# Wide token projections with tokens stationary and 512 weight columns moving, and a gated sum that is transposed

## The chip, the core and the metric

The kernel runs on one core of one Trainium2 chip. The metric is the device time of one execution in microseconds (us). Three runs of the kernel before gave 2199.41, 2200.2 and 2200.22 us.

## What is computed

Two layers of a first block (256 tokens, width 1024), each a token mixer and then a feed-forward net (dense in the first layer, 8 experts with top 2 in the second), and two hybrid layers behind it. All is float32. What the change touches:

```python
def token_mixer(...):             # layer a0, a1
    z = xn @ w_in                 # 7168 columns: pool, conv, sgu, q k v, 4 x 1024 gates
    ...                           # y_a, y_b, y_c: 256 wide; y_d (attention): 512 wide
    gates = sigmoid(z[..., OFF_GATE:])
    merged = (gates[:, :, 0] * (y_a @ w_branch_pool) + gates[:, :, 1] * (y_b @ w_branch_conv)
              + gates[:, :, 2] * (y_c @ w_branch_sgu) + gates[:, :, 3] * (y_d @ w_branch_attn))
    return merged @ w_out

def hybrid_layer(x, mem, ...):    # layer b0, b1
    proj = rmsnorm(x, pre_g) @ w_in          # 13 parts; z, sb_v, ret_v, ret_g are 512 wide
    y_ret = retention(ret_q, ret_k, ret_v) * silu(ret_g)
    y_ssd = ssd_mixer(xbc, z, ...); y_sb = stick_breaking(...) * silu(sb_g)
    y_mem = memory_read(mem_q, rmsnorm(mem), w_mem_kv) * silu(mem_g)   # keys, values: 512 wide each
    return x + rmsnorm(concat(y_ret, y_ssd, y_sb, y_mem) @ w_out, post_g)
```

## The kernel before

The program is a stream of weight tiles of [128, 2048] float32 (1 MB) in a fixed order (`weight_plan`), in the stages a0, ffn, a1, moe, b0, b1. Each is loaded by a DMA of SP, and split in two: H = the tile rounded to fp32r (ACT, `wh`), L = tile - H (DVE, `wl`). The activations are split likewise. A product is three fp32r matmuls: H by H, L by H, H by L. Tiles split ahead lie in a ring of three pairs of H and L; `ahead` issues the next tile's H in the middle of a tile and `lows` its L at the tile's end, so that a DVE queue reads: L of the next tile, then what empties the present one.

A tile is used in one of two ways. In `proj_w` the weights are stationary and 256 tokens move (`mm_w`): out is [columns, tokens]. In `proj_t` the tokens are stationary and 256 weight columns move (`mm_t`): out is [tokens, columns]. A tile holds all 8 row blocks of 256 columns and takes 48 matmuls of 256 columns, into one PSUM bank. `mm_t` is also used with 512 columns moving, by the sums over w_out, w_down and the like (`add`, `tail`).

PSUM has 8 banks in four rings of two: "ps" (the stream's projections, in turn), "ac" and "ad" (side work, sums), "tr" (transposes).

A layer of the first block (`layer_a`): the tile sv, emptied by a gelu of ACT; q, k, v by two tiles each (`proj_t`), emptied by a scaled copy of ACT; su, pa, cc, ch, cb (`proj_w`); then the gates of the four branches, four tiles each (`proj_w`, tanh on ACT), with the branches' own products between them. `branch(b)` multiplies (tanh + 1) by the product (DVE) and adds it to `mg` (GpSimd; in the last branch two of four on DVE). `mg` has columns on the partitions, so that each of its quarters is split (H, L) as it stands, one quarter behind the other, and becomes the moving side of w_out. The short convolution: zc = cc * ch, three taps into yc, yc * cb, all on DVE but one tap.

A layer of the second block (`layer_b`): z (2 tiles, `proj_t`), x, then in the order `sq sk mq sv rq rk rv sg mg rg` two tiles each; sv and rv by `proj_t`, the rest by `proj_w`. The gate of the retention, rg, has columns on the partitions, and multiplies the transposed result out of PSUM.

The memory's values (`mem_kv`, parts 2 and 3, `proj_t`) are a filler: their tiles run on PE at the start of moe and of b1, while the norm and the router are worked out. At the start of moe PE takes, between matmuls of these tiles: 16 transposes of x, the router's 16 matmuls (`ac<-hT,grw`), two small transposes of its logits (`tr<-cst,lT`), ten small ones with the masks (`tr<-sm,cst`), and then the gather of the first expert's tokens (`tr<-sel,xr`).

Attention, pooling, the gating unit and so on are side work: generators whose steps `tick` puts into the queues between the matmuls, where a rough model of the engines (`Clock`) expects their operands. So where a step stands may change with anything ahead of it.

Of the kernel before, what the change touches and what calls it, by code (L numbers as in the profile page):

```python
# [23 lines left out]
# for the bits of -v / 2: its sign and its exponent are in the shifted bits  # L24
MAGIC = 1597463007 + (1 << 30) - (1 << 22)

# ---------------------------------------------------------------- layouts by shape
# columns of "cols" (one value per partition)
# [31 lines left out]
# rows that are sent to all partitions  # L60
# [6 lines left out]
# constants  # L67
# [5 lines left out]
def _constants():  # L73
# [11 lines left out]
    # part A: 1/count of the pooling windows, the exchange matrix, one-hot buckets  # L85
# [15 lines left out]
    # part B: decays of the retention and the rotary tables  # L101
# [18 lines left out]
# ---------------------------------------------------------------- order of the weights  # L120
def _rg(a, n):
    return [(a, a + n)]


def weight_plan():
    """Tiles of [128, 2048] in the order of use: (array, index, first row block, row blocks, column ranges)."""
# [12 lines left out]
    def layer_a(l):  # L139
        put(("a", l, "sv"), "w_in", (l,), 0, 8, _rg(1280, 256))  # L140
        for nm, c0 in (("q", 1536), ("k", 2048), ("v", 2560)):
            for i in range(2):
                put(("a", l, nm, i), "w_in", (l,), 0, 8, _rg(c0 + 256 * i, 256))
# [3 lines left out]
        def gates(b):  # L147
            for i in range(4):
                put(("a", l, "g", b, i), "w_in", (l,), 0, 8, _rg(3072 + b * 1024 + 256 * i, 256))
# [20 lines left out]
    def memkv(l, *parts):  # L170
        for p in parts:
            put(("b", l, "mkv", p), "w_mem_kv_2", (l,), 0, 8, _rg(256 * p, 256))

    def layer_b(l):
        def p(nm, i, c0):
            put(("b", l, nm, i), "w_in_2", (l,), 0, 8, _rg(c0 + 256 * i, 256))
# [46 lines left out]
# where in the last expert the memory is taken up again  # L223
LATE = 3
KV0 = (0,), (1,), (2, 3)
IN_COLUMNS = dict(sq=3592, sk=4104, sv=4616, rq=0, rk=512, rv=1024, mq=5640, sg=5128, rg=1536, mg=6152)
IN_ORDER = "sq sk mq sv rq rk rv sg mg rg"
# [7 lines left out]
# ---------------------------------------------------------------- order of the side work  # L235
# [10 lines left out]
class Clock:  # L246
    """A rough clock of the engines while the program is traced: it says when an operand will be there, so that
    side work is put into the queues at a place where it doesn't hold up the stream of the weights."""
# [33 lines left out]
    def when(self, needs):  # L282
        """needs: operands, or "tag" / "tag2" for one or two free banks"""
# [70 lines left out]
# ---------------------------------------------------------------- the program  # L354
class Prog:
# [19 lines left out]
    # ---- small helpers  # L375
# [10 lines left out]
    def psb(self, tag):  # L386
        """a bank; "ac": of both rings in turn, while these aren't apart"""
# [18 lines left out]
    def rsqrt(self, src, n, scale, eng=None):  # L406
        """1 / sqrt(src * scale + eps), by Newton's steps"""
# [23 lines left out]
    def split(self, src, scale=None):  # L431
        """H + L of src [128, 512] * scale, both fp32r."""
        H, L = self.h(F32R, "sH"), self.h(F32R, "sL")
        self.split_to(H, L, src, scale)
        return H, L
# [9 lines left out]
    # ---- side work: generators that advance between the matmuls of the stream. They yield the operands that their  # L445
    # next step takes from other engines (or False while there is nothing to do yet).
# [5 lines left out]
    def step(self, t):  # L452
        """one step of a task; False if it can't go on yet"""
# [22 lines left out]
    def until(self, cond):  # L476
        """the steps that it takes until cond() holds"""
# [10 lines left out]
    # ---- the stream of the weights: tiles as they are, in a ring or wherever there is room, then as H and L  # L488
# [62 lines left out]
    def ahead(self, n=None, later=False):  # L551
        """splits the next n tiles (as many as fit beside the one in use), loads the ones behind them.
        later: the last one's L waits for lows(), so that DVE doesn't wait for H"""
# [34 lines left out]
    def next_steps(self):  # L588
        """the split of the next tile, in four parts"""
# [20 lines left out]
    def mm_w(self, out, W, X, nk, ncols, c0, k0=0, start=True, stop=True):  # L610
        """out [128 columns, 256 tokens] += W[:, c0:c0+128]^T x^T"""
# [11 lines left out]
    def mm_t(self, outs, W, X, nk, ncols, t, k0=0, start=True, stop=True, c0=0):  # L623
        """outs[i] [128 tokens of t, <=512 columns] += x W; the columns of the outs follow each other"""
# [17 lines left out]
    def four_apart(self):  # L642
        """four others; "ac" and "tr" stay free for side work"""
# [3 lines left out]
    def add(self, acc, key, X, k0=0, start=False):  # L647
        """acc[tokens][columns] += x W for 256 of the rows of W"""
# [9 lines left out]
    def tail(self, acc, steps, after):  # L658
        """the last of those sums, (key, X, k0) each: one half of the tokens first, then the other. Yields a half
        when it is done. after: how many tiles behind them are split before."""  # L660
# [40 lines left out]

    def keep(self, ps, name):
# [4 lines left out]
    def transposed(self, blocks, tag="tr"):  # L707
        """a bank of four transposed [128, 128] blocks"""
# [5 lines left out]
    # ---- rms norm of [256, 1024] rows; transposed, as H and L  # L714
    def norm_rows(self, x, rows):
        """adds to x what rows gives; each half's rows normalised"""
# [22 lines left out]
    def start_T(self, x, g):  # L739
        """for the first layer: the rows transposed before their norm, their scales, and after them, in steps,  # L740
        the rows with their norm"""
# [45 lines left out]
    def finish_T(self, block, g, X, tags=("tr", "tr")):  # L787
        """the transposed rows, two banks at a time: an engine takes one while the other has the other"""
# [23 lines left out]
    # ---- set up  # L812
# [25 lines left out]
    def load_row(self, src, n):  # L838
        """src: a row of n*512 values in DRAM, sent to all partitions."""
# [8 lines left out]
    # ---- first block  # L848
# [1265 lines left out]
```

## Time and profile before

| | us |
|---|---|
| median of three runs | 2200.2 |
| span of the profiled execution | 2197.8 |
| PE busy in it | 2173.0 (99%) |
| DVE busy | 1693.3 (77%) |
| ACT busy | 1398.2 (64%) |
| GpSimd busy | 139.0 (6%) |
[...]
| bytes moved by DMA | 558 MB, 254 GB/s in the mean |

The profiled execution is told by its span, 2.4 us below the median. Busy times of PE are sums of durations that overlap; the pace of matmuls is read from start to start. In the rows of the timeline a bracket at the end gives the time that the engine was idle before the instruction, and what released it. All instructions carry the line of one recording helper (L320), so they are told apart by the names of what they write and read.

### The profile page before, as it was taken

The numbers are of one execution on the slowest core, as the hardware profiler recorded it, in microseconds if no ns is written. First come the engines' busy times: TensorE is split into PE (matmuls) and PEld (weight loads), VectorE is DVE, ScalarE is ACT, GpSimd is POOL, SyncE is SP. The second block draws the span as 40 slices with busy tenths as digits, with TensorE's granted clock in tenths as the row PEclk, the third lists the DMA queues.
The fourth block names the chain that finished last, engine by engine and source line by source line (L and its number), as shares of the span: only waits on it lengthen the run. The fifth ranks groups of instructions, "written<-read, shape, count | busy, mean of one in ns | idle before, by whom it ended". The sixth has DMA issues, their size and how long they took to land. (4 is left out here: it accounts for less than half of the span.)

```text
span 2197.8 us, 34889 instructions
## 1 busy us (share of the span) xinstructions
PE 2173.0 (99%) x13470; PEld 1944.1 (88%) x13470; DVE 1693.3 (77%) x2242; ACT 1398.2 (64%) x1869; POOL 139.0 (6%) x159
## 2 busy tenths in 40 slices
PE   8999999999999999999999999999999999999998
PEld 8999999999998888888888888888877999989997
DVE  6675755567657889898989989898998767777765
ACT  6644544465445777777778777777776656455652
POOL 2003000100030000000000000000000022101300
PEclk9999999999999999999999999999999999999999
DMA  7445455544467999999999999999966444544342
GB/s 285 154 172 192 174 190 192 197 171 159 167 229 296 371 353 355 353 357 353 369 344 355 370 356 356 346 361 355 365 267 256 172 151 154 182 154 168 121 136 103
DMA packets 138140, 558.39 MB, mean 254 GB/s; under 512 B 15720, under 2 KB 16112, under 8 KB 88816
## 3 DMA queue, kind: packets, MB, share of 16 engines
q1 hardware_dynamic: 134928, 547.63, 68.0%
q0 software_dynamic: 2176, 6.90, 0.9%
q8 instruction: 108, 1.77, 0.3%
q10 hardware_dynamic: 864, 1.57, 0.2%
q14 instruction: 64, 0.52, 0.1%
HBM read 554.98 MB, written 1.06 MB: 253 GB/s over the span
## 5 line engine op out<-in xcount | busy, mean ns | idle before, releaser
L320 DVE TENSOR_TENSOR wl<-w,wh 128x2048 fp32r<-128x2048 f32 (+1 forms) x300 | 682.0, 2275 | 213.6 <-ACT wh L320 209.5
L320 ACT ACTIVATE wh<-w 128x2048 fp32r<-128x2048 f32 (+1 forms) x300 | 567.0, 1892 | 73.5 <-issue 36.1
L320 PE MATMUL ps<-xH,wh 128*128 128x256 f32 x1728 | 493.7, 286 | 2.1 <-PEq L1433 2.1
L320 PE MATMUL ps<-xL,wh 128*128 128x256 f32 x1728 | 489.3, 283 | 0.6 <-issue 0.4
L320 PE MATMUL ps<-xH,wl 128*128 128x256 f32 x1728 | 489.0, 283 | 0.1
L320 PE MATMUL ps<-wh,sH 128*128 128x512 f32 x944 | 377.0, 403 | 0.0
L320 PE MATMUL ps<-wh,sL 128*128 128x512 f32 x944 | 366.4, 392 | 0.0
L320 PE MATMUL ps<-wl,sH 128*128 128x512 f32 x944 | 364.8, 390 | 0.0
L320 PEld LDWEIGHTS ps<-xH,wh 128*128 128x128 f32 x1728 | 331.3, 192 | 5.2 <-issue 3.8
L320 PEld LDWEIGHTS ps<-xL,wh 128*128 128x128 f32 x1728 | 331.4, 192 | 1.6 <-DVE xL L320 0.8
L320 DVE TENSOR_TENSOR wl<-wraw,wh 128x512 fp32r<-128x512 f32 x536 | 331.2, 687 | 1.7 <-ACT wh L320 1.6
L320 PEld LDWEIGHTS ps<-xH,wl 128*128 128x128 f32 x1728 | 331.2, 192 | 0.9 <-issue 0.5
L320 ACT ACTIVATE wh<-wraw 128x512 fp32r<-128x512 f32 x536 | 293.2, 622 | 10.3 <-PE ac L320 10.2
L320 DVE TENSOR_TENSOR wl<-wm,wh 128x2048 fp32r<-128x2048 f32 x88 | 201.6, 2291 | 27.1 <-ACT wh L320 25.5
L320 PEld LDWEIGHTS ps<-wh,sL 128*128 128x128 f32 x944 | 177.1, 188 | 39.3
L320 PEld LDWEIGHTS ps<-wl,sH 128*128 128x128 f32 x944 | 177.8, 188 | 34.3 <-DVE wl L320 0.4
L320 PEld LDWEIGHTS ps<-wh,sH 128*128 128x128 f32 x944 | 177.3, 188 | 33.0
L320 ACT ACTIVATE wh<-wm 128x2048 fp32r<-128x2048 f32 x88 | 168.5, 1916 | 16.6 <-PE ac L320 12.4
L320 PE MATMUL ad<-wh,a 128*128 128x512 f32 x448 | 174.6, 390 | 1.8 <-DVE a L320 1.3
L320 PE MATMUL ac<-wh,a 128*128 128x512 f32 x448 | 174.3, 389 | 0.0
L320 PE MATMUL ps<-wh,xH 128*128 128x256 f32 x448 | 130.2, 291 | 1.3 <-ACT wh L320 1.3
L320 PE MATMUL ps<-wl,xH 128*128 128x256 f32 x448 | 128.9, 288 | 2.1 <-DVE wl L320 2.0
(436 smaller groups left out, 3053.8 us busy)
## 6 DMA issues: line engine op xcount, KB each, us to landing
w<-in_wts_dram SPq DMA_DIRECT2D x296, 1024.0 KB, 4.9
wraw<-in_wts_dram SPq DMA_DIRECT2D x536, 256.0 KB, 6.2
wm<-in_wts_dram SPq DMA_DIRECT2D x88, 1024.0 KB, 5.4
mem<-in_mem_dram POOLq DMA_DIRECT2D x12, 256.0 KB, 5.7
x<-in_x_dram SPq DMA_DIRECT2D x2, 512.0 KB, 4.5
w<-in_wts_dram SPq DMA_DIRECT2D x4, 256.0 KB, 7.3
br<-scr POOLq DMA_DIRECT2D x4, 256.0 KB, 7.1
row<-in_post_dram ACTq DMA_DIRECT2D x4, 256.0 KB, 5.3
```

The source lines that it names most:

```text
L320: r = f(*args, **kw)
```

## The change

q, k, v, the gates, z, sv, rv, rg and the memory's values now use `proj_t2`: tokens stationary, 512 weight columns moving. Two tiles make up what two tiles did, but each holds 4 row blocks of 512 columns. Both "ps" banks are held, one for each half of the tokens (t), and are written in turn, 12 matmuls each: t 0 and t 1 by the first tile, t 0 and t 1 by the second. The banks are emptied behind the second tile. The branches' tiles go the same way (24 matmuls of 512 columns), so `mg` has tokens on the partitions. All four additions of the last branch are on DVE. `turned` transposes the sum, column half by column half, 8 transposes each, and splits it out of PSUM: the first half behind branch 3, the second behind the first w_out tile. The retention's gates are multiplied before the transposes. attn scales q and k in one step.

```diff
+    def proj_t2(self, key, X, tag="ps"):
+        ps = [self.psb(tag) for _ in range(2)]
+        for i in range(2):
+            W = self.W(key + (i,))
+            for t in range(2):
+                self.mm_t([ps[t]], W, X, 4, 512, t, k0=4 * i, start=i == 0, stop=i == 1)
+                if t == 0:
+                    self.ahead(later=True)
+                    if i == 0:
+                        self.tick()
+            self.lows()
+            if i == 0:
+                self.tick()
+        return ps
...
         def gates(b):
-            for i in range(4):
-                ps = self.proj_w(("a", l, "g", b, i), X)
-                th[b, i] = self.h(F32, "th")
-                S.activation(th[b, i], ps, AF.Tanh, scale=0.5)
+            for j in range(2):
+                for t, ps in enumerate(self.proj_t2(("a", l, "g", b, j), X)):
+                    th[b, j, t] = self.h(F32, "th")
+                    S.activation(th[b, j, t], ps, AF.Tanh, scale=0.5)
                 self.tick()
+        def turned(j):
+            for kp in range(2):
+                ps = self.transposed([mg[j][t][:, (2 * kp + kk) * 128:(2 * kp + kk) * 128 + 128]
+                                      for kk in range(2) for t in range(2)])
+                M.append(self.split(ps, scale=0.5))
         def branch(b):
             self.until(lambda: b in self.Y)
...
+            def gated(j, t, ps):
+                t_ = th.pop((b, j, t))
                 V.scalar_tensor_tensor(t_, t_, 1.0, ps, op0=ALU.add, op1=ALU.mult)
...
-                    (V if b == 3 and i > 1 else G).tensor_tensor(mg[i], mg[i], t_, op=ALU.add)
-                if i == 1 or b == 3 and i == 3:
-                    self.ahead()
-                if b == 3 and i:
-                    mg[i - 1] = self.split(mg[i - 1], scale=0.5)
-            if b == 3:
-                mg[3] = self.split(mg[3], scale=0.5)
+                    (V if b == 3 else G).tensor_tensor(mg[j][t], mg[j][t], t_, op=ALU.add)
...
+            else:
+                for j in range(2):
+                    W = self.W(("a", l, "b", b, j))
+                    for t in range(2):
+                        ps = self.psb("ac" if t else "ps")
+                        self.mm_t([ps], W, self.Y[b], 4, 512, t)
+                        gated(j, t, ps)
+                        if t == 0:
+                            self.ahead(later=True)
+                    self.lows()
+                    if j == 1:
+                        turned(0)
...
         for i in range(n):
-            self.add(acc, ("a", l, "o", i), M, 2 * i, start=i == 0)
+            self.add(acc, ("a", l, "o", i), self.halves(M[i]), start=i == 0)
+            if i == 0:
+                turned(1)
...
     def mem_kv(self, l, *parts, tag="ps"):
         for p in parts:
             self.until(lambda: l in self.XM)
-            ps = (self.proj_w if p < 2 else self.proj_t)(("b", l, "mkv", p), self.XM[l], tag)
-            self.kv[l, p] = self.keep(ps, "mkv")
+            if p < 2:
+                self.kv[l, p] = self.keep(self.proj_w(("b", l, "mkv", p), self.XM[l], tag), "mkv")
+            elif p == 2:
+                for mb, ps in enumerate(self.proj_t2(("b", l, "mkv", 2), self.XM[l], tag)):
+                    self.kv[l, 2 + mb] = self.keep(ps, "mkv")
```

Three places show how the change stands in the queues. First, DVE at the end of branch 3 in layer a0, where `th` is a product or a sum of the branches, `wl` the L of a weight tile and `sL` that of a quarter of the sum. Before:

```order
L320 SCALAR_TENSOR_TENSOR sL_2555<-th_1277,sH_2554 128x512
L320 SCALAR_TENSOR_TENSOR th_2373<-th_2373,ad_2558 128x512
L320 TENSOR_TENSOR th_1470<-th_1470,th_2373 128x512
L320 TENSOR_TENSOR wl_2586<-w_2310,wh_2585 128x2048
L320 SCALAR_TENSOR_TENSOR sL_2592<-th_1357,sH_2591 128x512
L320 SCALAR_TENSOR_TENSOR sL_2596<-th_1470,sH_2595 128x512
```

and now:

```order
L329 SCALAR_TENSOR_TENSOR th_1785<-th_1785,ps_1893 128x512
L329 TENSOR_TENSOR th_1231<-th_1231,th_1785 128x512
L329 SCALAR_TENSOR_TENSOR th_1787<-th_1787,ad_1911 128x512
L329 TENSOR_TENSOR th_1233<-th_1233,th_1787 128x512
L329 TENSOR_TENSOR wl_1909<-w_1753,wh_1908 128x2048
L329 SCALAR_TENSOR_TENSOR sL_1935<-tr_1929,sH_1934 128x512
L329 SCALAR_TENSOR_TENSOR sL_1944<-tr_1938,sH_1943 128x512
```

The first quarters' L stood ahead of the branch's last product; now the first L of the sum, which the first w_out tile reads, stands behind the last product, its addition and the L of a weight tile.

Second, DVE around the tile cb in layer a0 (`p` and `sm` are softmax, `zc` and `yc` the convolution, `ps` in the row of `yc` the tile cb). Before, where the L of cb stands further ahead, in front of a division:

```order
L320 SCALAR_TENSOR_TENSOR p<-ac,B 128x512
L320 TENSOR_REDUCE sm<-p 128x2
L320 SCALAR_TENSOR_TENSOR p<-ad,B 128x512
L320 TENSOR_REDUCE sm<-p 128x2
L320 TENSOR_TENSOR wl<-w,wh 128x2048
L320 TENSOR_TENSOR zc<-cs,ps 128x2x256
L320 SCALAR_TENSOR_TENSOR yc<-zc,cols,yc 128x256 x4
L320 TENSOR_TENSOR wl<-w,wh 128x2048
L320 TENSOR_TENSOR yc<-yc,ps 128x512
```

and now:

```order
L329 SCALAR_TENSOR_TENSOR p<-ad,B 128x512
L329 TENSOR_REDUCE sm<-p 128x2
L329 SCALAR_TENSOR_TENSOR p<-ac,B 128x512
L329 TENSOR_REDUCE sm<-p 128x2
L329 TENSOR_TENSOR wl<-w,wh 128x2048 x2
L329 TENSOR_TENSOR zc<-cs,ps 128x2x256
L329 SCALAR_TENSOR_TENSOR yc<-zc,cols,yc 128x256 x4
L329 TENSOR_TENSOR wl<-w,wh 128x2048
L329 TENSOR_TENSOR yc<-yc,ps 128x512
```

The L of cb has moved behind the third set of logits, so that two Ls stand there; ahead of these rows the order also has the gating unit's product now, which stood far behind before.

Third, PE at the start of moe, around the small transposes with the masks. Before:

```order
L320 MATMUL ps_7286<-wl_7214,xH_2630 128x256
L320 MATMUL ps_7286<-wh_7213,xL_2631 128x256
L320 MATMUL tr_7305<-sm_7258,cst_79 128x8 x5
L320 MATMUL ps_7286<-wh_7213,xH_2628 128x256
L320 MATMUL ps_7286<-wl_7214,xH_2628 128x256
L320 MATMUL ps_7286<-wh_7213,xL_2629 128x256
```

and now:

```order
L329 MATMUL ps_5899<-wh_5926,xH_1978 128x512
L329 MATMUL ps_5899<-wl_5927,xH_1978 128x512
L329 MATMUL ps_5899<-wh_5926,xL_1979 128x512
L329 MATMUL tr_6045<-sm_6006,cst_79 128x8 x5
L329 MATMUL tr_6059<-sel_6056,xr_5814 128x128
L329 MATMUL tr_6059<-sel_6056,xr_5815 128x128
```

30 matmuls of the filler followed the small transposes before the gather; now the gather follows them directly.

## Rows read from the trace of the kernel before

**Rows 1.** The page, part 1: busy us, share of the span, instructions.
```profile
PE 2173.0 (99%) x13470; PEld 1944.1 (88%) x13470; DVE 1693.3 (77%) x2242; ACT 1398.2 (64%) x1869; POOL 139.0 (6%) x159
```

**Rows 2.** Pieces of the chain that ended last: start, length, engine, tile, count.
```profile
1750.36 23.03 PE ps L320 x192
...
1773.39 0.87 PE tr L320 x8
...
2181.25 8.17 PE ps L320 x36
```

**Rows 3.** The page, part 5: group, out<-in, shapes, count, busy, mean ns, idle.
```profile
L320 PE MATMUL ps<-wh,sH 128*128 128x512 f32 x944 | 377.0, 403 | 0.0
```

**Rows 4.** Timeline at sv and q, layer a0: start, length, engine (PE, ACT), instruction.
```profile
18.93 0.28 PE L320 MATMUL ps<-wh,xH 128*128 128x256 f32 x1
...
22.35 0.84 ACT L320 ACTIVATE vg<-ps,sm 128x256 f32<-128x256 f32 x2
```

**Rows 5.** Timeline of DVE, layer a0, from cc to cb.
```profile
78.89 0.69 DVE L320 SCALAR_TENSOR_TENSOR p<-ac,B 128x512 f32<-128x512 f32 x1 [1.62 <-PE ad L320]
...
81.54 0.23 DVE L320 RECIPROCAL sm<-sm 128x4 f32<-128x4 f32 x2
...
84.28 2.29 DVE L320 TENSOR_TENSOR wl<-w,wh 128x2048 fp32r<-128x2048 f32 x1
86.48 0.22 DVE L320 RECIPROCAL sm<-sm 128x2 f32<-128x2 f32 x2
...
88.45 0.69 DVE L320 SCALAR_TENSOR_TENSOR p<-ac,B 128x512 f32<-128x512 f32 x1
...
98.97 0.68 DVE L320 TENSOR_TENSOR yc<-yc,ps 128x512 f32<-128x512 f32 x1
```

**Rows 6.** Timeline of PE, layer a0: a logit pair up to the next matmul; first gates matmul.
```profile
77.72 0.48 PE L320 MATMUL ac<-qkT 64*128 64x256 f32 x1
...
78.80 0.39 PE L320 MATMUL ps<-xH,wh 128*128 128x256 f32 x1
...
94.56 0.28 PE L320 MATMUL ps<-xH,wh 128*128 128x256 f32 x1
```

**Rows 7.** Timeline of layer a1: zc and yc on DVE, first gates matmul on PE.
```profile
524.31 0.68 DVE L320 TENSOR_TENSOR zc<-cs,ps 128x512 f32<-128x512 f32 x1
...
526.53 0.28 PE L320 MATMUL ps<-xH,wh 128*128 128x256 f32 x1
...
529.98 0.68 DVE L320 TENSOR_TENSOR yc<-yc,ps 128x512 f32<-128x512 f32 x1
```

**Rows 8.** Timeline of DVE, layer a0, at the end of branch 3.
```profile
224.29 0.68 DVE L320 SCALAR_TENSOR_TENSOR th<-th,ad 128x512 f32<-128x512 f32 x1
225.01 0.69 DVE L320 TENSOR_TENSOR th<-th 128x512 f32<-128x512 f32 x1
225.62 2.28 DVE L320 TENSOR_TENSOR wl<-w,wh 128x2048 fp32r<-128x2048 f32 x1
227.82 1.29 DVE L320 SCALAR_TENSOR_TENSOR sL<-th,sH 128x512 fp32r<-128x512 f32 x2
```

**Rows 9.** Timeline of PE and DVE at the start of moe.
```profile
686.19 0.28 PE L320 MATMUL tr<-cst,lT 8*128 8x8 f32 x2
...
688.20 2.73 DVE L320 SCALAR_TENSOR_TENSOR xr<-x,sm,row 128x512 f32<-128x512 f32 x4
690.85 2.28 DVE L320 TENSOR_TENSOR wl<-wm,wh 128x2048 fp32r<-128x2048 f32 x1
...
693.99 2.48 DVE L320 TENSOR_TENSOR wl<-wraw,wh 128x512 fp32r<-128x512 f32 x4
...
694.81 1.61 PE L320 MATMUL tr<-sel,xr 128*128 128x128 f32 x13
```

**Rows 10.** Start of b1: timeline of PE; a stretch's busy us, PEclk, DMA share.
```profile
1955.81 0.63 PE L320 MATMUL tr<-cst,xr 128*128 128x128 f32 x4 [1.59 <-DVE xr L320]
...
1959.00:1961.00 2.00, 2.00 (x11) 2.00 (x11) 1.85 (x5) 1.78 (x6) 0.00 (x0) 0.50 0.71 291
```

## What is predicted, before it ran

> **What bounds the kernel now.** I read the page's busy shares first: PE is busy 99% of the span [rows 1]. A busy PE need not be at its pace, since its matmul durations overlap, so the second view is the chain of work that ended last, which in the stages that the change touches runs through PE almost alone. Its merged pieces give the pace from start to start: 192 matmuls of 256 columns in 23.03 us, 0.120 us each; 36 of 512 columns in 8.17 us, 0.227 us each; 8 transposes in 0.87 us, 0.11 us each [rows 2]. The 512-column form in the stage of that piece is one of tokens stationary and weights moving already (its group is in [rows 3]), so the form that the change brings has its pace in this trace. Third, I read the timelines of DVE, ACT and PE where the tiles of the change begin and end, for what stands between a tile's last matmul and the freeing of its PSUM bank. PE hardly waits there now, so what the change takes off PE comes off the time, and each wait that it makes is added in full.
>
> **The matmuls.** A 1 MB tile was 48 matmuls of 256 columns: 48 x 0.120 = 5.76 us. It is now 24 of 512: 24 x 0.227 = 5.45 us. Per layer that holds for 6 tiles of q, k, v, 16 of gates, 5 of branches, 8 of z, sv, rv, rg and 2 of memory values: 37, in two layers 74. 74 x 0.31 = 22.9 us less. [...] Bytes, DMA issues and the splits by ACT (H) and DVE (L) are the same in number. The transposed sum adds 16 transposes per layer, 32 x 0.11 = +3.5 us on PE. First balance: **-19.4 us**.
>
> [...]
>
> **What the change makes PE wait for.** A pair of tiles holds both "ps" banks from its first 2.72 us (12 matmuls) on. The bank used last before it was needed again after 5.76 us, now after 2.72 us. Most tiles are emptied within a microsecond by one ACT or DVE instruction. These places are not:
>
> - sv to q, first layer: q's first matmul starts at 18.93, and the gelu that empties sv's bank ends at 22.35 + 0.84 = 23.19 [rows 4], since it waits for the norm's scale. The bank is now wanted at 18.93 + 2.72 = 21.65: **+1.5 us**. Nothing in that chain moves.
> - cb to gates, both layers. cb is multiplied into yc by DVE, behind a 2.28 us L of the next tile; that ends 98.97 + 0.68 = 99.65, 5.1 us after cb [rows 5, 6], in the second layer 4.1 us after it [rows 7]. With 2.72 allowed, 2.4 and 1.4 us are the plain extrapolation. But the order also puts softmax later against the tiles and, in the first layer, the sgu work earlier. From the middle of pa's tile on DVE has there: three sets of logits (2.65 each, 78.89 to 81.54), two divisions (2.74 and 1.97), the sgu product (some 1.5, an estimate from its two shapes) and two Ls (2.2 each), 18.6 us from 1.2 us on, to 19.8 us [rows 5]. PE has in the meantime three logit pairs (1.08 each [rows 6]), sgu (some 1.1), two and a half tiles of 5.76: 18.8 us, and then wants cb's L: about +0.9. Next comes zc, behind one more L of DVE, whose H stands on ACT behind the last exponentials and a copy: some 3.6 us after the third logits at 17.6 (an estimate), so L 21.2 to 23.4 and zc at 23.4; from zc to the end of yc are 6.35 us (524.31 to 530.66 [rows 7]), so 29.7; wanted at 18.8 + 0.9 + 5.8 + 2.7 = 28.2: +1.5. In the second layer the second logits come half a tile later than before, at 10.8 us after su; 14.4 us of the same pieces follow, zc at 25.2, end 31.6; cb ends at 26.3 (three and a half tiles, three pairs, from the same rows: 20.2 + 3.2, and 2.9 of the half tile), so wanted at 29.0: +2.6. Together **+5.0 us** (0 to 7).
> - Branch 3 to the first w_out tile, both layers. Now three quarters of the sum are split when branch 3 ends, and PE goes on at once. After it, w_out needs the transposed sum split as L, and DVE has in front of that: product, sum and a 2.28 us L (as in [rows 8]). From the end of branch 3: 0.2 (the way to DVE, an estimate) + 0.72 + 0.61 + 2.20 + 0.65 = 4.4 us. PE fills 0.9 with 8 transposes (counted above) and 0.9 with the four matmuls that want H alone: 4.4 - 1.8 = 2.6, with the semaphore 2.7. Twice: **+5.4 us**. The nearest cover would be an L that is through before (then 0.5 each); at the other end 3.5 each.
> - Start of moe. The router's masks follow the small transposes at 686.19, and 30 matmuls of the second memory tile stood between the next small ones and the selection; DVE's rows of xr (2.7 us), an L, and the selection were hidden by them [rows 9]. Now 36 matmuls of 512 stand ahead of 686.19 (8.2 instead of 4.3 us: 690.0) and only 12 behind it. DVE: 688.20 + 3.85 = 692.05, xr to 694.7, an L in four pieces (2.48) to 697.2, selection 0.94: 698.1. PE is there at 690.2 + 2.7 + 1.1 (ten small ones at 0.11) = 694.0: **+4.1 us** (2 to 6).
> [...]
> - Start of b1: the two value tiles only fill the wait for the norm, which ends when it ends [rows 10]: their gain of **0.6 us** is not had.
> - Retention's gates are now multiplied before the transposes (8 small instead of 4 wide DVE instructions, far ahead of their use), attn scales q and k together, and one branch's additions go from POOL to DVE while DVE has room: nothing, covered by PE's next tiles; if the cover is gone, one eviction, about 1 us. Side work that the planner puts elsewhere: **+1.0 us** (-1 to +3).
>
> Sum: -19.4 + 1.5 + 5.0 + 5.4 + 4.1 + 1.3 + 0.6 + 1.0 = **-0.5 us**. The span was 2197.8, so 2197.3; the median lay 2.4 above the profiled span, so **2199.7 us**: no change that can be measured (a measurement of this kernel tells 0.2%, 4.4 us, from none).
>
> **Rivals.**
> (A) The waits come only in part: DVE is less behind than I count, so that cb and the router find their operands. For it: DVE is busy 77% and stands idle before many Ls for ACT. Against it: the queues are strictly in the order shown. Without cb, moe and its clock: -19.4 + 1.5 + 5.4 + 0.6 = -11.9, so 2188; with no wait at all 2181. Chance 0.25.
> (B) Slower: the second bank of every pair comes late. The place is the end of all 32 pairs (16 per layer; the branches are no pairs), the price the time by which its eviction passes 2.72 us. Without sv, cb and the unknown 1.0 the sum is -8.0 us, so it decides from 8.0 / 32 = 0.25 us per pair; at 0.5 us it is +8.0, so 2208. For it: an L of 2.28 us ahead of an eviction of 0.7 alone ends 3.2 us after the tile. Against it: most evictions are ACT's, and their L is through before the tile ends. Chance 0.17.
> (C) The change does not shorten the matmuls: if time went by columns alone, 512 would take 2 x 0.120 and only the costs would stay, 3.5 + 1.5 + 5.0 + 5.4 + 4.1 + 1.3 + 1.0 = +21.8: 2222. The two paces speak against it [rows 2]. [...] Chance 0.03.
> The forecast keeps 0.55.
>
> **How the numbers follow.** Likeliest: 2199.7. The single costs add to about -7 and +7 at their bounds, hardly all at one end. With 0.25 on A, whose times lie at 2181 to 2195, and 0.20 on B and C, the range of 8 in 10 is 2191 to 2207. Faster by over 0.2%: 0.25 (A); within: 0.55; slower: 0.20 (B, C).
>
> **What would show it.** In the changed profile: 12 matmuls of 512 columns in 2.72 us in q, gates and z (else the first term is wrong); idle PE of 1.5 us in q's first tile, released by ACT's gelu; of some 2.5 us at cb and the first gates, released by DVE; of 2 us and more four matmuls into the first w_out tile, released by sL; of 4 us ahead of the selection's transposes, released by sel, with a granted clock of 0.5 behind it. I am wrong if PE's busy time fell by much more than it waits (A), or if "ps" matmuls wait at most pairs (B).

## The result, and the profile of the changed kernel

The changed kernel took **2211.7 us** in the median (2210.2 to 2214.6) against 2200.2 before: 1.0055 of its time, 95% interval 1.0040 to 1.0069. It is slower, and lies 4.7 us above the range that was predicted. The profiled execution has a span of 2210.2 us, 12.4 more than the 2197.8 of before.

The first row below is PE's share on the page (as in [rows 1]): 6.2 us less busy, and yet a longer span. The second is the stretch in which PE runs the four gate tiles of one branch in layer a0, all of the new form (the columns are those of the table of stretches below; x97 counts one matmul that reaches in from before). The first of their 96 matmuls of 512 columns starts at 152.12, and what follows them at 173.88: 21.76 us, 0.227 us each as in [rows 2], 5.44 us a tile, at the full clock. So the tiles did become shorter by what was worked out.

```profile
PE 2166.8 (98%) x11726; PEld 1859.4 (84%) x11726; DVE 1694.6 (77%) x2250; ACT 1398.1 (63%) x1863; POOL 121.7 (6%) x155
```

```profile
152.12:173.88 21.76, 21.76 (x97) 18.02 (x96) 11.10 (x7) 9.36 (x7) 0.00 (x0) 1.00 0.55 194
```

PE's starts at the borders of the stages, read from its timeline, say where the time went. The last column is what the terms of the prediction make of each stage, without the 1.0 us of side work that it gave no place.

| stage | before us | after us | difference | terms on record |
|---|---|---|---|---|
| first mixer (first w_in matmul to ffn) | 235.81 | 237.05 | +1.24 | 0.0 |
| ffn | 201.55 | 201.62 | +0.07 | 0 |
| second mixer | 228.67 | 230.21 | +1.54 | -1.3 |
| start of moe, to the first gathered tokens | 30.48 | 35.57 | +5.09 | +4.8 |
| experts, to b0's transposes | 999.26 | 1000.41 | +1.15 | 0 |
| b0, to b1's transposes | 247.12 | 247.54 | +0.42 | -2.5 |
| b1, to PE's end | 235.84 | 238.74 | +2.90 | -2.5 |
| together | | | +12.41 | -1.5 |

Next are all the places in the timeline of PE, from the second tile on, where the changed kernel waits over 1.2 us, but for the starts of b0 and b1 (z, and b1's transposes). Those wait nearly as long in the kernel before, z there in five short pieces. The columns are start, length, instruction and, in brackets, the idle time ahead of it and what ended it. (That idle time counts from a matmul's modelled end. From start to start, beyond the pace, the waits are some 0.16 to 0.2 us longer: 2.17 us for the row with 2.00. The text gives these.)

```profile
23.22 0.50 PE L329 MATMUL ps<-wh,xH 128*128 128x512 f32 x1 [1.49 <-ACT vg L329]
...
99.84 0.50 PE L329 MATMUL ps<-wh,xH 128*128 128x512 f32 x1 [1.29 <-DVE yc L329]
...
222.88 0.50 PE L329 MATMUL ac<-wh,sL 128*128 128x512 f32 x1 [2.00 <-DVE sL L329]
...
530.66 0.68 PE L329 MATMUL ps<-wh,xH 128*128 128x512 f32 x1 [2.23 <-DVE yc L329]
531.14 0.63 PE L329 MATMUL ps<-wl,xH 128*128 128x512 f32 x1
531.57 0.63 PE L329 MATMUL ps<-wh,xL 128*128 128x512 f32 x1
532.00 0.63 PE L329 MATMUL ps<-wh,xH 128*128 128x512 f32 x1
...
655.61 0.50 PE L329 MATMUL ac<-wh,sL 128*128 128x512 f32 x1 [2.00 <-DVE sL L329]
...
701.00 2.25 PE L329 MATMUL tr<-sel,xr 128*128 128x128 f32 x11 [3.78 <-DVE sel L329]
...
1707.80 0.36 PE L329 MATMUL ps<-xH,wh 128*128 128x256 f32 x1 [2.29 <-PEq L1487]
...
1856.35 0.39 PE L329 MATMUL ps<-xH,wh 128*128 128x256 f32 x1 [1.67 <-ACT rv L329]
...
2107.14 0.39 PE L329 MATMUL ps<-xH,wh 128*128 128x256 f32 x1 [1.73 <-ACT rv L329]
```

The first six are those of the prediction, each at its place, by its releaser and nearly at its size: sv to q 1.65 (1.5 predicted), cb 1.45 and 2.39 (2.4 and 2.6), the transposed sum 0.47 + 2.17 in both layers (2.7), the selection 3.92 (4.1). The seventh, the branch ahead of the last part of moe, was there before. The last two, at the pair of rv in each hybrid layer, nobody had counted.

The second thing to see is in the three rows behind 530.66: matmuls of 512 columns start 0.43 us apart, not 0.227. The table of stretches has the granted clock behind seven waits (columns: stretch, its length, busy us of PE, PEld, DVE, ACT, POOL, granted clock, DMA share, GB/s):

```profile
224.00:227.00 3.00, 3.00 (x11) 2.41 (x11) 0.00 (x0) 0.00 (x0) 0.00 (x0) 0.50 0.73 306
531.00:534.00 3.00, 3.00 (x8) 2.32 (x8) 1.59 (x2) 2.07 (x2) 0.00 (x0) 0.50 0.92 317
658.00:660.00 2.00, 2.00 (x6) 1.61 (x5) 0.35 (x1) 0.00 (x0) 0.00 (x0) 0.50 1.05 396
702.00:704.00 2.00, 2.00 (x11) 2.00 (x11) 0.00 (x0) 0.00 (x0) 0.00 (x0) 0.50 1.05 385
1709.00:1711.00 2.00, 2.00 (x11) 2.00 (x11) 0.67 (x4) 2.00 (x5) 0.00 (x0) 0.50 1.04 434
1968.00:1971.00 3.00, 3.00 (x8) 2.28 (x9) 2.70 (x8) 2.66 (x7) 0.00 (x0) 0.50 0.74 232
2108.00:2111.00 3.00, 3.00 (x14) 3.00 (x15) 2.02 (x1) 2.65 (x2) 0.00 (x0) 0.50 0.66 221
```

The kernel before has, after its first 16 us, one such stretch, at b1's start [rows 10]. The changed one has seven. A busy PE hides this: it reads 3.00 of 3.00 us busy there, with 8 matmuls of 512 columns where 13 would fit.

So the theory to test was: **the saving was had, the waits came as worked out, two more came at rv, and six more stretches at half clock, at some 1 to 1.75 us each, are what the sum lacked.** Its rivals: the waits are not what sets the time (DVE or ACT is the bound there, and a wait taken away comes back one tile later), or the clock falls for another reason than the waits.

### The profile page after: what moved, and what is told of

The parts are those of the page before. It is cut to its first block, busy times and chain, and to the rows that moved or that the text cites. A ratio compares the mean times of both kernels' runs of the same rounds, so it can differ in the third digit from the quotient of the medians.

```text
span 2210.2 us, 31406 instructions
## 1 busy us (share of the span) xinstructions
PE 2166.8 (98%) x11726; PEld 1859.4 (84%) x11726; DVE 1694.6 (77%) x2250; ACT 1398.1 (63%) x1863; POOL 121.7 (6%) x155
## 3 DMA queue, kind: packets, MB, share of 16 engines
q8 instruction: 94, 1.54, 0.3%
## 5 line engine op out<-in xcount | busy, mean ns | idle before, releaser
L329 PE MATMUL ps<-wh,sH 128*128 128x512 f32 x976 | 389.9, 403 | 0.0
L329 PE MATMUL ps<-xH,wh 128*128 128x256 f32 x1152 | 331.2, 288 | 5.7 <-ACT rv L329 3.4
L329 PE MATMUL ps<-xH,wl 128*128 128x256 f32 x1152 | 327.7, 284 | 0.5 <-DVE wl L329 0.5
L329 PE MATMUL ps<-xL,wh 128*128 128x256 f32 x1152 | 327.6, 284 | 0.2
L329 PEld LDWEIGHTS ps<-xH,wh 128*128 128x128 f32 x1152 | 222.1, 193 | 9.7 <-ACT rv L329 4.2
L329 PEld LDWEIGHTS ps<-xL,wh 128*128 128x128 f32 x1152 | 222.2, 193 | 1.5 <-DVE xL L329 0.8
L329 PEld LDWEIGHTS ps<-xH,wl 128*128 128x128 f32 x1152 | 222.2, 193 | 1.1 <-DVE wl L329 1.1
L329 PE MATMUL ps<-wh,xH 128*128 128x512 f32 (+1 forms) x528 | 207.9, 394 | 7.2 <-DVE yc L329 3.5
L329 PE MATMUL ps<-wl,xH 128*128 128x512 f32 (+1 forms) x528 | 205.2, 389 | 2.8 <-DVE wl L329 2.7
L329 PE MATMUL ps<-wh,xL 128*128 128x512 f32 (+1 forms) x528 | 204.7, 388 | 0.0
L329 ACT ACTIVATE wh<-wm 128x2048 fp32r<-128x2048 f32 x88 | 168.3, 1914 | 15.4 <-PE ac L329 12.4
```

What stands on the lines that cost most here:

```text
L329: r = f(*args, **kw)
```

## The experiments

Each of the first seven takes the changed kernel and takes something away. All stand against 2211.7 us (changed) and 2200.2 (before).

### Taking one wait away at a time

**The sum turned earlier.** Half 0 of the gated sum is whole when half 1 begins. Here it is transposed and split there.

```
@@ branch 3
                         if t == 0:
+                            if j == 1:
+                                turned(0)
                             self.ahead(later=True)
                     self.lows()
-                    if j == 1:
-                        turned(0)
```

> The changed kernel with one edit: in branch 3 the first half of the sum is transposed and split between the two halves of the last tile, not after it, so that its H and L stand ahead of the 2.28 us L of a weight tile on DVE. In the changed kernel PE waited 0.47 + 2.17 us (first layer, at 219.1 and 220.5) and 0.47 + 2.16 us (second layer) there, and the granted clock was 0.50 for some 3.4 us behind each, which cost about 1.75 us more each. Theory (the waits are real, and a wait of this length also costs the clock): both go, 2 x (2.64 + 1.75) = 8.8 us less than the changed kernel: 2203 us (2202 to 2204.5), and no clock of 0.50 at the start of w_out. Rival 1 (only the wait comes back; the slow stretch behind it has another cause, such as the DMA or the new tiles): 5.3 us less, 2206.4, with the clock still at 0.50. Rival 2 (DVE is the bound there, so the wait only moves to the L of the next weight tile): 2210 to 2212.

Measured: 2203.4 us (2200.6 to 2205.1), 8.3 less. DVE's timeline shows why. In the changed kernel the L of a weight tile stood ahead of the sum's L:

```profile
219.93 2.28 DVE L329 TENSOR_TENSOR wl<-w,wh 128x2048 fp32r<-128x2048 f32 x1
222.14 1.28 DVE L329 SCALAR_TENSOR_TENSOR sL<-tr,sH 128x512 fp32r<-128x512 f32 x2
```

With the edit the order is the other way round (DVE's timeline), PE works without a wait of over 0.2 us through both ends of branch 3, and the clock stays up (stretches, columns as above):

```profile
218.00 1.28 DVE L329 SCALAR_TENSOR_TENSOR sL<-tr,sH 128x512 fp32r<-128x512 f32 x2
...
220.84 2.28 DVE L329 TENSOR_TENSOR wl<-w,wh 128x2048 fp32r<-128x2048 f32 x1
```

```profile
216.00:224.00 8.00, 8.00 (x44) 6.75 (x43) 7.50 (x10) 5.80 (x7) 0.00 (x0) 1.00 0.39 133
640.00:660.00 20.00, 20.00 (x98) 16.71 (x97) 15.38 (x15) 8.16 (x8) 0.00 (x0) 1.00 1.02 382
```

The waits alone would be 5.3 us. The rest came back with the clock, so both rivals fall here. Elsewhere the clock of this execution was not that of the changed kernel's: it did not fall at cb in the second mixer, and fell for twice as long behind the selection (688 to 695 us).

**cb copied out by ACT**, so that its bank no longer waits for DVE's queue.

```
-        ps = self.proj_w(("a", l, "cb"), X)
-        V.tensor_tensor(yc, yc, ps, op=ALU.mult)
+        cb = self.keep(self.proj_w(("a", l, "cb"), X), "cb")
+        V.tensor_tensor(yc, yc, cb, op=ALU.mult)
```

> The changed kernel with one edit: ACT copies cb's bank out, and DVE's product with yc reads the copy, so that the bank is free without DVE's queue. In the changed kernel the first gates waited 1.45 us for that bank in the first layer and 2.39 + 0.25 us in the second, the second with a clock of 0.50 behind it (about 1.4 us). Theory: the bank is free about a microsecond after cb's last matmul, 1.45 + 2.64 + 1.4 = 5.5 us less than the changed kernel: 2206.2 (2205 to 2208). Rival (ACT's queue is as late as DVE's, or the side work that the planner now puts elsewhere costs as much): 2209 to 2213.

Measured: 2207.1 us (2205.2 to 2208.8), 4.6 less. PE has no wait over 0.2 us left at cb in either layer, so the bank it was. In this execution the clock fell for twice as long behind the selection (693 to 701 us), and once behind rv in b0, where it had not fallen in the changed kernel.

**The memory values undone**, with the fillers around the router as before.

```
-            if p < 2:
-                put(("b", l, "mkv", p), "w_mem_kv_2", (l,), 0, 8, _rg(256 * p, 256))
-            else:
-                put(("b", l, "mkv", 2, p - 2), "w_mem_kv_2", (l,), 4 * (p - 2), 4, _rg(512, 512))
+            put(("b", l, "mkv", p), "w_mem_kv_2", (l,), 0, 8, _rg(256 * p, 256))
...
-            elif p == 2:
-                for mb, ps in enumerate(self.proj_t2(("b", l, "mkv", 2), self.XM[l], tag)):
-                    self.kv[l, 2 + mb] = self.keep(ps, "mkv")
+            ps = (self.proj_w if p < 2 else self.proj_t)(("b", l, "mkv", p), self.XM[l], tag)
+            self.kv[l, p] = self.keep(ps, "mkv")
```

> The changed kernel with one part undone: the memory values of both layers are again two tiles of 256 columns, each with its own bank, so that the fillers around the router stand as in the kernel before. Four tiles lose 0.32 us each, two of them in places that only fill a wait. Theory (the 3.9 us wait for the selection and the slow clock behind it come from the order of these tiles): the stretch from the first of these tiles to the first gathered tokens returns from 35.6 to 30.5 us, the start of b1 stays: 2206.6 (2205.5 to 2208). Rival (the router is late for another reason, such as the end of the mixer's w_out): the wait stays and 0.6 to 1.3 us of saving is lost, 2212 to 2213.

Measured: 2206.5 us (2202.6 to 2207.8), 5.2 less. In PE's timeline the selection's 32 transposes run through with no idle time ahead of them:

```profile
697.30 3.74 PE L326 MATMUL tr<-sel,xr 128*128 128x128 f32 x32
```

From the first small transposes (680.24) to the first gathered tokens (709.29) this kernel needs 29.05 us, just as the kernel before (677.75 to 706.80). The wait was the order of these tiles and nothing else. Here too the clock fell in other places than in the changed kernel: for twice as long behind w_out in the first mixer (222 to 230 us), and not behind it in the second.

### The pair of rv

What holds PE at 1856.35? First ACT's timeline, then DVE's, of the changed kernel. rv's last matmul starts at 1854.30.

```profile
1847.66 1.90 ACT L329 ACTIVATE wh<-w 128x2048 fp32r<-128x2048 f32 x1
...
1850.55 1.28 ACT L329 ACT_TABLE_LOAD   x1
1851.84 1.77 ACT L329 ACTIVATE spl<-spl 128x384 f32<-128x384 f32 x4
1853.51 0.51 ACT L329 ACTIVATE spH<-spl 128x384 fp32r<-128x384 f32 x1
1853.93 1.90 ACT L329 ACTIVATE wh<-w 128x2048 fp32r<-128x2048 f32 x1
1855.73 1.06 ACT L329 ACTIVATE rv<-ps 128x512 f32<-128x512 f32 x2
```

```profile
1846.56 0.55 DVE L329 SCALAR_TENSOR_TENSOR lt<-ac,masks 128x384 f32<-128x384 f32 x1
1852.39 1.97 DVE L329 SCALAR_TENSOR_TENSOR spl<-lt,spl 128x384 f32<-128x384 f32 x4 [5.29 <-ACT spl L329]
1854.28 0.55 DVE L329 TENSOR_TENSOR spL<-spl,spH 128x384 fp32r<-128x384 f32 x1
1854.75 4.49 DVE L329 TENSOR_TENSOR wl<-w,wh 128x2048 fp32r<-128x2048 f32 x2
```

The logarithms of the stick-breaking branch (spl, with a table load of 1.28 us) stand in the second tile of this pair. On ACT they and an H of 1.90 us are ahead of the copies that free the banks. The same chain was there in the kernel before, in rv's first tile (ACT's timeline of before):

```profile
1839.05 1.77 ACT L320 ACTIVATE spl<-spl 128x384 f32<-128x384 f32 x4
...
1841.13 1.90 ACT L320 ACTIVATE wh<-w 128x2048 fp32r<-128x2048 f32 x1
1842.93 0.57 ACT L320 ACTIVATE rv<-ps 128x512 f32<-128x512 f32 x1
```

That copy ended 2.7 us after the last matmul of its tile (PE goes on at 1840.83), and it cost nothing, because the bank was wanted only a whole tile later. Now the chain comes one tile later against PE, and the first bank is wanted 2.7 us after its last matmul. The first run only moved the first copy ahead of the H:

```
+    def proj_t2_early(...):          # proj_t2, but yields each bank when its matmuls are queued
...
+                if i == 1:
+                    yield ps[t]
                 if t == 0:
                     self.ahead(later=True)
...
-                    for ps in self.proj_t2(("b", l, nm), X):
+                    for ps in (self.proj_t2_early if nm == "rv" else self.proj_t2)(("b", l, nm), X):
```

> The changed kernel with one edit: the first bank of the retention's values (rv) is copied by ACT as soon as its last matmul is queued, ahead of the 1.89 us H of the next weight tile, not behind it. In the changed kernel the pair of rv was followed by waits of 1.83 + 0.39 us in b0 and 1.89 + 0.39 + 0.26 us in b1, the latter with a clock of 0.50 behind it (about 1.5 us). Theory (second bank of a pair comes late because ACT has a chain of 4.5 us of side work and then an H ahead of the copy): the bank is free some 1.9 us earlier, about 0.2 to 0.6 us of wait is left in each, the clock stays up: 1.7 + 2.0 + 1.5 = 5 us less than the changed kernel, 2206.5 (2205.5 to 2208). Rival 1 (the wait alone): 3.6 less, 2208. Rival 2 (ACT is the bound: H comes 0.57 us later and PE waits for the weights instead): 2210 to 2212.

Measured: 2210.0 us (2208.6 to 2211.2), only 1.7 less, which the spread of the two kernels does not tell from nothing. My theory of this wait fell, by the trace. The banks were free, and PE waited as long for the next tile's L instead, in b0 as in b1 (timeline of PE):

```profile
1851.79 0.39 PE L329 MATMUL ps<-xH,wl 128*128 128x256 f32 x1 [2.02 <-DVE wl L329]
...
2104.04 0.39 PE L329 MATMUL ps<-xH,wl 128*128 128x256 f32 x1 [2.02 <-DVE wl L329]
```

The rows of DVE above had shown it: DVE is idle for 5.29 us ahead of the products that take ACT's logarithms, and the L of the next tile, whose H was ready at 1847.66 + 1.90 = 1849.56, stands behind them in its queue. `proj_t2` lets side work in between a tile's H and its L; what comes in there and waits for ACT holds up the L. So the second run closes that gap for rv as well:

```
 proj_t2_early, used for rv only
                 if t == 0:
                     self.ahead(later=True)
-                    if i == 0:
-                        self.tick()
```

> The changed kernel with the pair of rv mended in both places: its first bank is copied as soon as its matmuls are queued (as in the run before that did only this), and side work may no longer be queued between the H and the L of the next weight tile, so that DVE's L does not stand behind products that wait for ACT's logarithms (DVE idle 5.3 us ahead of them in the changed kernel). With the first edit alone PE waited 2.18 us for that L in both layers, in place of the bank. Theory (two engines' queues hold that pair, ACT's the bank and DVE's the L): with both freed the wait falls below 0.5 us in both layers, and no clock of 0.50 stands behind it: 1.9 + 2.1 + 1.5 = some 5.5 us less than the changed kernel's 2211.7, 2206 (2204.5 to 2208). Rival (stick's chain of 4.5 us on ACT has no cover at this place, the wait goes on to the next tile): 2209.5 to 2212.

Measured: 2205.0 us (2202.0 to 2206.1), 6.7 less. Both rv waits are gone. In their place one of 0.97 us in each layer ([0.80] in the timeline of PE), where rv's own pair needs a bank that DVE is still taking rk from:

```profile
1842.78 0.50 PE L329 MATMUL ps<-wh,xH 128*128 128x512 f32 x1 [0.80 <-DVE rk L329]
```

Two queues held that pair, each long enough to hide the other. (No run has the second edit alone.) The waits saved come to some 2.7 us. The rest is the clock, which in this execution was at 0.50 behind three waits, not seven. Two of the four that it lacks are in the second mixer, which the edit does not touch.

### Together

This run has the four edits whose diffs stand above: the sum turned earlier, cb copied out, the memory values undone, and rv's pair with both its edits.

> The changed kernel with four edits together: the transposed sum early (8.3 us less when alone), cb copied by ACT (4.6 less), the memory values undone (5.2 less), rv's pair mended as in the run beside this (5.5 by its theory). Theory (the costs are waits at separate places of PE, so what they give adds up): 2211.7 - 23.6 = 2188 (2186 to 2193), faster than the kernel before by 0.5%, and the granted clock at 0.50 in no more places than in the kernel before. Rival (DVE and ACT have no room: as PE comes earlier everywhere, waits appear at other places): 2195 to 2200.

With the four edits: **2189.3 us** (2188.3 to 2191.7), 0.9956 of the time before (0.9939 to 0.9972). The four alone sum to 24.8 us less, together they give 22.4. The waits were nearly additive. The first balance of the prediction, -19.4, is not reached (-10.9): left are sv's 1.7, rv's 2 x 0.97, the undone tiles' 1.3, a slow stretch of 1.0 at the end of moe, a wait of 1.5 for the L of b1's z (at 1954.51), which neither the kernel before nor the changed one has, and short waits. Then the last of the predicted waits, at sv:

```
-            ps, o = self.proj_t(key, X), self.h(F32, name)
+            ps, o = self.proj_t(key, X, "ps" if scales is None else "ac"), self.h(F32, name)
```

> As the run with the four edits, and the bank of sv in the first layer is taken from the ring that the side work uses, so that q's pair finds both of its banks free (1.65 us of wait at 21.4 in the changed kernel, for the gelu that waits for the norm's scale). Theory: 1.65 us less than with the four edits, 2186.5. Rival (what PE gains there it waits for at the next norm's transposes, which set that stretch): no less than with the four edits, 2188.

Measured: 2191.6 us (2191.0 to 2193.1), 2.3 **more** than without it, though the highest time without it (2191.7) is above the lowest here. The wait at q went, but `psb("ac")` deals from ac and ad in turn, and one bank more at the start exchanged the two for all that came after. In each hybrid layer (b0 at 1885.67, b1 at 2136.39) w_out then waits for a bank that DVE is still multiplying with a gate (s):

```profile
1885.67 0.50 PE L326 MATMUL ad<-wh,yH 128*128 128x512 f32 x1 [1.54 <-DVE s L326]
...
2136.39 0.51 PE L326 MATMUL ad<-wh,yH 128*128 128x512 f32 x1 [1.54 <-DVE s L326]
```

The last run names the ring, so that the turn stays ("ad" for "ac" in the line above):

> The four edits together (2189.3), and the bank of sv in the first layer taken from the ring ad by name, so that the two rings of the side work keep their turns. When the bank came out of both rings in turn, the wait at q went (1.72 us) but PE waited 1.8 us at a w_out of each hybrid layer, where a bank was found in the other ring than before, and the time was 2191.6. Theory (it was the exchanged turn): the wait at q goes, none comes at these two places, 1.7 us less than with four edits: 2187.6. Rival (a bank less in the side work's rings at the start is what costs): 2189 to 2192.

Measured: **2187.8 us** (2187.3 to 2189.3), 0.9945 of the time before (0.9929 to 0.9962). Neither wait is there, so it was the exchanged turn. This is the lowest median of the study: 12.4 us below the kernel before, 23.9 below the changed one. The 1.5 us to the run with four edits is inside the spread of both, so it is the wait that is shown to be gone, not the gain in time. Its PE row and the one stretch at half clock that it has after the start, behind the branch at moe's end:

```profile
PE 2156.4 (99%) x11822; PEld 1857.4 (85%) x11822; DVE 1694.7 (78%) x2250; ACT 1398.5 (64%) x1865; POOL 121.0 (6%) x155
```

```profile
1689.00:1692.00 3.00, 3.00 (x16) 3.00 (x16) 1.61 (x10) 2.92 (x5) 0.00 (x0) 0.50 1.00 421
```

### A wait by itself

Three runs take the kernel *before*, where nothing of the change is, and put one wait into its dense ffn. They do spare work that the result does not need.

```
@@ ffn, loop over f
+            if f == 11:
+                self.G.tensor_tensor(z[:, 0:256], z[:, 0:256], g[:, 0:256], op=ALU.add)
+                for _ in range(4):                     # 4, 5, 6
+                    self.G.tensor_tensor(z, z, z, op=ALU.add)
+            if f == 12:
+                self.T.transpose(pz[:, 0:128], z[:, 0:128], self.ident)
```

> The kernel before, and one wait put into its quiet stretch, the dense ffn: after one of its tiles GpSimd adds a spare tile to itself once on 256 and four times on 512 columns (about 0.7 + 4 x 1.29 us by the rope products in the trace of before), beginning when ACT's silu is there, and PE transposes the result one tile (5.76 us) later. So PE should wait about 0.8 us. Theory (a short wait costs what it lasts): wait and transpose, about 1 us, and no granted clock of 0.50 behind it: 2201 us. Rival (any wait costs the clock): 1.7 us more, 2203.

> As the run beside it with five such additions, so that PE should wait about 2.1 us. Theory (the waits of the changed kernel over 2 us cost their length and some 1.7 us of clock in most executions): 2.2 + 1.7 us, 2204, with the granted clock at 0.50 for about 3.4 us behind the wait. Rival (the clock fell in the changed kernel for another reason than the wait, such as its new tiles or their DMA): 2.2 us, 2202.4, clock at its upper level throughout.

> As the run beside it with six such additions, so that PE should wait about 3.4 us. Theory: 3.5 + 1.7 us, 2205.4, the clock at 0.50 for about 3.4 us behind the wait. Rival (clock not by the wait): 3.5 us, 2203.7.

In each of the three one of GpSimd's additions took 2.97 us, the others 1.0 to 1.2. So all three waits came 1.2 to 1.4 us longer than planned, and all three times lie above what was expected. The transpose in the timeline of PE, and the stretch behind it, for four, five and six additions:

```profile
360.01 0.33 PE L320 MATMUL tr<-cst,zz 128*128 128x128 f32 x1 [2.06 <-POOL zz L320]
```

```profile
361.00:364.00 3.00, 3.00 (x15) 2.46 (x14) 2.29 (x1) 0.64 (x1) 0.00 (x0) 1.00 0.74 311
```

```profile
360.44 0.33 PE L320 MATMUL tr<-cst,zz 128*128 128x128 f32 x1 [3.30 <-POOL zz L320]
```

```profile
361.00:364.00 3.00, 3.00 (x10) 2.37 (x9) 2.15 (x1) 0.00 (x0) 0.00 (x0) 0.59 0.47 197
```

```profile
361.38 0.33 PE L320 MATMUL tr<-cst,zz 128*128 128x128 f32 x1 [4.42 <-POOL zz L320]
```

```profile
361.00:364.00 3.00, 2.62 (x8) 2.07 (x9) 2.47 (x1) 0.00 (x0) 0.32 (x1) 0.62 0.39 164
```

Behind the waits of 3.3 and 4.4 us the clock falls to 0.50 (the 0.59 and 0.62 are means of stretches that take in the full clock too), and eight matmuls of 512 columns then start 0.427 us apart, 1.6 us lost. With nothing of the change in the program, its tiles or DMA can't be the reason: the wait is. Behind the 2.06 us it did not fall.

The stages say where these executions are longer than that of the kernel before. The ffn is longer by 2.4, 5.3 and 6.4 us: the wait (2.2, 3.5 and 4.6 from start to start), the transpose and, for the two longer waits, the slow stretch. The experts are longer by 3.3, 2.0 and 2.1: at the end of moe the branch waits 3.3 to 3.5 us (2.3 before), and the clock falls behind it, which it did not in the profile of before; in the first of the three it stays down for 7 us. Why the branch waits longer there is not shown. The medians, 2205.2, 2206.8 and 2208.2, are 4.8 to 7.8 us above the 2200.4 of the kernel before beside them.

For the two longer waits this bears the theory out. For the shortest, which came out as long as the waits of the changed kernel, the one execution that was profiled shows no price beyond its length. The ten times of that kernel lie in two groups, 2203.5 to 2203.7 and 2205.1 to 2205.8, 1.6 us apart, about what one slow stretch costs. But the profiled execution is of the upper group, so the groups can't be put down to a stretch behind this wait.

## Why the prediction was wrong, point by point

- **The matmuls: right.** 5.44 us per tile where 5.45 was worked out. What two matmuls of 256 columns take beyond one of 512 was what the trace of before said: 2 x 0.120 - 0.227 = 0.013 us [rows 2], 24 x 0.013 = 0.31 us a tile.
- **The single waits: right.** 14.7 us measured (1.65, 1.45 + 2.39, 2 x 2.64, 3.92) where 16.0 stood in the sum. The largest miss is cb in the first layer, 1.45 for 2.4. Each went when its cause was taken away, and none came back one tile on.
- **The clock: this step failed.** The sum has 1.3 us for it, behind one wait, moe's. No run shows that term. Behind six waits more than before it fell to 0.50, at 1.75 (w_out, first mixer), 1.5 and 1.6 (cb and w_out, second mixer), 1.7 (selection), 1.0 (end of moe) and 1.5 us (rv in b1): 9.0 in place of 1.3. These are PE's starts beyond the pace of the whole stretch. The rows that warn of it were there: one wait of 1.59 us in b1 with 0.50 behind it [rows 10], and five new waits of over 2 us in my own list. The 1.3 was my estimate from that stretch in b1, a poor place for a price: in the runs with four and five additions to the kernel before the clock does not fall at b1's start, and b1 is as long (235.77 us) as with the fall (235.84), as PE waits there instead: with five additions it is idle for 1.0 us in all from 1963 to 1972. The 9.0 us are those of the profiled execution. Other executions have fewer or other slow stretches, but none of the four timed was under 2210.2.
- **Side work that moves: mis-sized.** It had +1.0 (to +3). At rv alone it cost 4.7 us of waits. I read the planner's moves where PE waited in the trace of before, not where its pieces land in a pair that has no second bank behind it. "Most tiles are emptied within a microsecond" left rv out of the list of slow ones, where its first copy took 2.7 us in the trace of before. Rival B had the mechanism, a pair whose bank comes late, but wanted it at all 32 pairs; two pairs, and a weight tile's L behind the same work, were enough.
- **Nothing for the retention's gates and q and k together: right.** No wait of the changed kernel stands there.

The two failed steps are +7.7 and +3.7 us, the smaller waits -1.3; that makes +10.1 of the 12.9 us by which the span (2197.3 on record) was missed. Most of the rest is short waits of 0.2 to 0.4 us in the hybrid layers, some 1 us in each beyond those of before. The last 0.8 I could not place.

That the range did not hold has one main reason: the single costs were summed at their middle, and the clock behind them, which has one sign and in this execution came with most of them, stood in the sum as one more small term.

## What to carry to other kernels

A wait on the bounding engine is not priced by its length alone where the clock may fall behind it: look in the trace of before for a wait with a lower granted clock behind it, and put the slow stretch (here 1 to 1.75 us) with a chance into the sum beside each wait of that size which the change makes. Where PE waited behind it anyway, at b1's start, it cost nothing (235.84 us with the fall, 235.77 without). When a tile's buffers are grabbed in pairs, look at what is queued between a tile's load and its use on *each* engine: taking away the wait that the profile names showed a second one of the same length behind it. And a saving that is lost to waits at separate places is worth mending place by place: here -19.4 us on PE became +11.5 in the time, and four small edits in the order of the work gave 22.4 of it back.

## What the runs showed of the hardware that I had not expected

The same wait does not always cost the clock. In the run with rv's first edit the sum's L and cb in the second mixer are waited for as long as in the changed kernel (the two rows of PE), and the clock stays up behind both (the stretches):

```profile
222.65 0.50 PE L329 MATMUL ac<-wh,sL 128*128 128x512 f32 x1 [2.00 <-DVE sL L329]
...
528.83 0.50 PE L329 MATMUL ps<-wh,xH 128*128 128x512 f32 x1 [2.23 <-DVE yc L329]
```

```profile
223.00:226.00 3.00, 3.00 (x19) 2.57 (x18) 0.23 (x2) 0.54 (x2) 0.00 (x0) 1.00 0.85 319
526.00:532.00 6.00, 3.77 (x18) 2.80 (x17) 4.19 (x4) 2.44 (x2) 0.00 (x0) 1.00 0.57 202
```

The executions of one kernel would fit that: the kernel before, with one slow stretch in its profile, lies within 2.1 us (2199.2 to 2201.3), the changed kernel with seven within 4.4, the one with the sum turned earlier within 4.5. It is a loose sign, as the run with four edits, with one, spreads over 3.4. In these runs a wait of some 2 us had a chance of a slow stretch, not a certainty. Why one wait is hit and another of the same length is not is not shown, and which waits of an execution will be hit stays open.
